# Projections of a hybrid decoder layer as a stage of their own, in seven products of halves, with attention and 22 gate chunks behind it

## The chip, the cores and the metric

The kernel runs on one core of one Trainium2 chip. The metric is device time in microseconds (us), the median of several executions. One more execution was recorded by the hardware profiler; its records are "the profile" or "the trace" here. The engines are PE (matrix products and transposes; PEld is its weight load), DVE, ACT and POOL (element-wise work), and SP, which issues most DMA transfers. ACT issues transfers too.

## The reference

One decoder layer on x of 1024 tokens by 1024 channels, float32:

```python
h = rms_norm(x, mix_norm_g)
proj = h @ w_in                      # 1024 x 8708: q, k, v of four mixers, 4 forget logits, 4 x 1024 gate logits
ys = four causal attentions of 4 heads of 64: stick-breaking (sb), dilated in 3 groups (dil),
     forgetting (fox), differential (dif)
branch = einsum('bsnc,ncd->bsnd', ys, w_branch)
x = x + sum(sigmoid(gates) * branch, axis=2) @ w_out
x = x + square(relu(rms_norm(x, mlp_norm_g) @ w_up)) @ w_down
return rms_norm(x, final_norm_g)
```

## The kernel before

**Numbers in two halves.** Every operand of a product is held as a rounded part `hi` and a rest `lo`. A product is three matmuls (`mm3`, L147 to L149): hi by hi, lo by hi, hi by lo. `wpiece` (L126, L127) makes hi and lo of a weight piece on POOL; in the MLP `split` (L966, L967) makes them on ACT and DVE.

**Stages.** (1) The normalised, transposed input `hTh`, `hTl` is made from eight tiles of x (`norm_transpose`, L178 to L186). (2) Twelve attention units run: dif 0 and 1, dil 0 to 2 with two head pairs each, fox 0 and 1, sb 0 and 1. Between them stand the projections of the next unit and the gate chunks. (3) The branch stage (`pb`) merges the four branches by gates, (4) `po` is w_out, (5) `pu` and `pd` are the MLP. The MLP already works in seven products of halves in place of eight (Strassen's scheme in Winograd's form; the table `PRODUCTS`).

**Projections.** `lin_T` makes 128 columns of q or k for all tokens: 2 halves of the tokens by 8 blocks of channels by 3 matmuls of width 512 (tile `lin`). `proj_v` makes 256 columns of v (tile `linv`, width 256). `gate_ahead` makes one of 32 gate chunks (tile `lg`, 48 matmuls of width 512) and stores it in DRAM (`gl`). q, k and v go from PSUM by `evac_hi` on ACT and `evac_lo` on DVE straight into the SBUF tiles that attention reads; only v of the dilated groups 1 and 2 goes by DRAM.

**Attention.** Per head and block of 128 queries: scores into PSUM (`sc`), a row operation on DVE (fox L576, dif L634, dil L704; sb: two sigmoids on ACT, L508 and L509, then a scan and a product on DVE, L510 and L513), `exp` on ACT, and then `pv`: transposes on PE (`pt`, L419), hi on ACT (L423), lo on DVE (L424), products with v on PE (`o`, L428 and L430). Fox also adds a row on POOL (L567) and scales by 1/sum on DVE (L583). The buffers are NS = 5 row tiles `s`, 2 PSUM tiles for scores, 2 for transposes, 1 for outputs.

**What sets the order.** The program is written unit by unit; `N_BEFORE`, `N_AFTER` and `N_MID` say how many gate chunks are written around each unit. The framework's scheduler then fixes one order per engine when the program is built, and each engine runs its list in that order. A chunk therefore need not stay where it was written.

Of the kernel before, what the change touches and what calls it, by code (L numbers as in the profile page):

```python
# [11 lines left out]
F32 = mybir.dt.float32  # L12
# [9 lines left out]
P = 128  # L22
# [20 lines left out]
N_BEFORE = (1, 4, 3, 3, 0, 0, 0, 0, 0, 1, 1, 0)  # L43
N_AFTER = (0, 1, 1, 0, 0, 0, 0, 0, 1, 0, 3, 9)
N_MID = (0, 4)
# [3 lines left out]
W_AT = 2  # L49

DW_AT = 2

UORDER = (0, 1, 2, 3, 4, 5)

ORDER_N = (3, 2, 1, 0)

NWR, NWH, NS, NPT, NQK = 4, 4, 5, 6, 12
# [4 lines left out]
def kernel(  # L62
# [111 lines left out]
    def norm_transpose(xt, rs, g_bc, t, hi, lo, xn, pspool, tag):  # L174

        if rs is None:
            rs = rms_rstd(xt, xn, D)
        nc.vector.scalar_tensor_tensor(xn, xt, rs, g_bc, op0=ALU.mult, op1=ALU.mult)  # L178
        for b in range(2):
            ps = pspool.tile([P, 4, P], F32, tag=tag, name=nm("nt"))  # L180
            for i in range(4):
                nc.tensor.transpose(ps[:, i], xn[:, (4 * b + i) * P:(4 * b + i + 1) * P], ident)
            oh = hi[:, 4 * b:4 * b + 4, t * P:(t + 1) * P]
            ol = lo[:, 4 * b:4 * b + 4, t * P:(t + 1) * P]
            nc.scalar.copy(oh, ps)
            nc.vector.tensor_sub(ol, ps, oh.bitcast(F32))  # L186

# [8 lines left out]
    hT_pool = tc.tile_pool(name="hT", bufs=1, side="right")  # L196
    hT_pool_c = ctx.enter_context(ExitStack())
    hTp = hT_pool_c.enter_context(hT_pool)
    hTh = hTp.tile([P, NK, T], F32R, name="hTh")
    hTl = hTp.tile([P, NK, T], F32R, name="hTl")  # L200


    with ExitStack() as actx:
# [6 lines left out]
        g_bc = ap_.tile([P, D], F32, tag="s", bufs=NS, name="g_bc")  # L210
        for t in range(NT):
            xt = ap_.tile([P, D], F32, tag="qk", bufs=NQK, name=nm("xt"))
            nc.sync.dma_start(xt, x[t * P:(t + 1) * P, :])
            if t == 0:
                nc.sync.dma_start(g_bc, mix_norm_g[0:1, :].to_broadcast([P, D]))
            if t == W_AT:
                ws_first = [wcols(w_in, (DIF_V, DIL_V, DIL_V + 256, DIL_V + 512, FOX_V, SB_V)[UORDER[0]], 256)]
            xn = ap_.tile([P, D], F32, tag="s", bufs=NS, name=nm("xn"))
            norm_transpose(xt, None, g_bc, t, hTh, hTl, xn, ps_t, "t")

# [45 lines left out]
        bf_row = const.tile([P, 4], F32, name="bf_row")  # L266
        nc.sync.dma_start(bf_row, b_forget[0:1, :].to_broadcast([P, 4]))
# [19 lines left out]


        plan, held = [], []

        def w_next(off, n):
            assert plan[0] == (off, n), (plan[0], off, n)
            plan.pop(0)
            return held.pop() if held else wcols(w_in, off, n)

        def w_prefetch():
            if plan and not held:
                held.append(wcols(w_in, *plan[0]))

        def lin_T(off, evac):  # L300
            ws = w_next(off, P)
            for th in range(2):
                ps = ps_lin.tile([P, 512], F32, tag="lin", name=nm("lin"))
                sl = slice(th * 512, th * 512 + 512)
                mm3(ps, [(ws[k], (hTh[:, k, sl], hTl[:, k, sl])) for k in range(NK)])
                with tc.high_priority(offset=EVAC_LEAD):
                    evac(th, ps)

        def order(ap, th, dil):

            if dil == 1:
                return ap[:, th * 512:(th + 1) * 512]
            n = 512 // dil
            return ap.rearrange("p (r n) -> p r n", r=dil)[:, :, th * n:(th + 1) * n]

        def src(ap, dil):
            if dil == 1:
                return ap
# [613 lines left out]

# [346 lines left out]
```

## Time and profile before

| | us |
|---|---|
| median of 3 runs (lowest, highest) | 1944.81 (1938.52, 1946.4) |
| profiled execution, its own time | 1943.38 |
| its span | 1941.2 |
| PE busy | 1849.6 |
| DVE, ACT, POOL busy | 1067.5, 829.6, 822.6 |

The profiled time is 2.2 us over its span and 1.4 us under the median. Matmuls overlap in the pipeline, so the mean duration of one is longer than the distance between two; the distance is what PE has to pay. A row of windows gives, for a stretch, its length, then busy time and count of PE, PEld, DVE, ACT, POOL, then the granted PE clock (1.00 is full), the share of the DMA engines and GB/s. In the groups `| a, b | c <-X d` means a us busy in total, b ns for one, c us idle of that engine before them, d of it ended by X.

### The profile page before, as it was taken

The page shows a single profiled execution, that of the slowest core. Times are in us where ns is not written, and L with a number is a line of the kernel's source. Part 1 is how long each engine was busy: PE and PEld are TensorE (multiplying, and loading weights), DVE is VectorE, ACT ScalarE, POOL GpSimd, SP SyncE. Part 2 cuts the span into 40 slices and gives each one's busy share as a digit, 9 for nine tenths or more (in the row PEclk, how much of TensorE's full clock was granted, in tenths as well). Part 3 has the DMA queues.
Part 4 walks back from the last instruction along what each step waited for, and adds up shares of the span by engine and source line. Part 5 has one row for each costly group of instructions (what it writes and reads, how often), then busy time and mean ns, then how long its engine had stood idle before and what let it go on. Part 6 is the DMA issues. An engine that isn't in the chain of part 4 may idle for free.

```text
span 1941.2 us, 27207 instructions
## 1 busy us (share of the span) xinstructions
PE 1849.6 (95%) x9635; PEld 1554.0 (80%) x9635; DVE 1067.5 (55%) x1872; ACT 829.6 (43%) x1709; POOL 822.6 (42%) x739
## 2 busy tenths in 40 slices
PE   7999999999999999999998799959999999999997
PEld 7888877888888889888886578948888887788885
DVE  5143464535444457586632684294455454859587
ACT  4133443445444344454422442255454544444354
POOL 4333244322222433332333673365565541617164
PEclk9999999999999999999998899979999999999999
DMA  4734113224242322222236953233535439665355
GB/s 146 165 93 125 49 49 88 61 86 137 60 143 62 82 60 68 55 56 66 77 93 195 302 168 138 88 114 134 165 130 165 134 120 367 213 187 179 109 175 184
DMA packets 205880, 246.99 MB, mean 127 GB/s; under 512 B 16816, under 2 KB 129840, under 8 KB 205744
## 3 DMA queue, kind: packets, MB, share of 16 engines
q1 hardware_dynamic: 166912, 168.52, 29.3%
q10 hardware_dynamic: 38832, 76.73, 11.8%
q8 instruction: 76, 1.25, 0.3%
q14 instruction: 60, 0.49, 0.1%
HBM read 166.38 MB, written 65.18 MB: 119 GB/s over the span
## 4 chain that ended last, share of the span: by engine, by line
PE 82%; DVE 6%; DMA 5%; issue 4%; POOL 2%; ACT 1%; SPq 0%; POOLq 0%; DVEq 0%; ACTq 0%
PE lg L147 6%; PE lg L148 6%; PE lg L149 6%; PE pu L1083 5%; PE pu L1084 5%; PE pu L1082 5%; PE lin L149 5%; PE lin L148 5%; PE lin L147 5%; PE pd L1187 5%; PE pd L1185 4%; PE pd L1186 4%; PE pt L419 3%; PE linv L148 2%; PE linv L147 2%
## 5 line engine op out<-in xcount | busy, mean ns | idle before, releaser
L126 POOL TENSOR_SCALAR wh<-wr 128x512 fp32r<-128x512 f32 (+1 forms) x168 | 114.6, 684 | 443.4 <-PE linv L149 144.3
L127 POOL TENSOR_TENSOR wl<-wr,wh 128x512 fp32r<-128x512 f32 (+1 forms) x168 | 233.8, 1395 | 9.1
L147 PE MATMUL lg<-hTh,wh 128*128 128x512 f32 x512 | 204.1, 399 | 2.6 <-ACT gs L483 2.6
L148 PE MATMUL lg<-hTl,wh 128*128 128x512 f32 x512 | 204.4, 399 | 0.0
L149 PE MATMUL lg<-hTh,wl 128*128 128x512 f32 x512 | 203.2, 397 | 0.0
L1185 PE MATMUL pd<-wh,sh 128*128 128x512 f32 x448 | 177.1, 399 | 3.6 <-ACT sh L966 3.5
L1186 PE MATMUL pd<-wl,sh 128*128 128x512 f32 x448 | 175.7, 396 | 0.0
L1187 PE MATMUL pd<-wh,sl 128*128 128x512 f32 x448 | 169.8, 397 | 3.5 <-DVE sl L967 3.5
L967 DVE TENSOR_TENSOR sl<-sr,sh 128x512 fp32r<-128x512 f32 x112 | 108.2, 966 | 84.8 <-ACT sh L966 84.4
L148 PE MATMUL lin<-hTl,wh 128*128 128x512 f32 x384 | 153.8, 401 | 0.0
L147 PE MATMUL lin<-hTh,wh 128*128 128x512 f32 x384 | 153.7, 400 | 0.0
L149 PE MATMUL lin<-hTh,wl 128*128 128x512 f32 x384 | 152.2, 400 | 0.0
L966 ACT CAST sh<-sr 128x512 fp32r<-128x512 f32 x112 | 69.4, 619 | 160.3 <-PE pd L1186 140.6
L424 DVE TENSOR_TENSOR ptl<-pt,pth 128x512 fp32r<-128x512 f32 (+2 forms) x168 | 99.4, 604 | 68.6 <-ACT pth L423 67.4
L423 ACT CAST pth<-pt 128x512 fp32r<-128x512 f32 (+2 forms) x168 | 85.1, 524 | 94.8 <-PE pt L419 90.4
L147 PEld LDWEIGHTS lg<-hTh,wh 128*128 128x128 f32 x512 | 96.6, 189 | 23.4 <-ACT gs L483 1.9
L147 PE MATMUL linv<-wh,hTh 128*128 128x256 f32 (+1 forms) x384 | 112.5, 295 | 1.8 <-POOL wh L126 1.7
L148 PE MATMUL linv<-wl,hTh 128*128 128x256 f32 (+1 forms) x384 | 112.4, 293 | 0.0
L149 PEld LDWEIGHTS lg<-hTh,wl 128*128 128x128 f32 x512 | 96.3, 188 | 19.9
L149 PE MATMUL linv<-wh,hTl 128*128 128x256 f32 (+1 forms) x384 | 111.7, 292 | 0.0
L148 PEld LDWEIGHTS lg<-hTl,wh 128*128 128x128 f32 x512 | 96.4, 188 | 18.8
L967 DVE TENSOR_TENSOR wl<-wq,wh 128x512 fp32r<-128x512 f32 x75 | 74.6, 994 | 56.5 <-ACT wh L966 55.2
(344 smaller groups left out, 4951.3 us busy)
## 6 DMA issues: line engine op xcount, KB each, us to landing
wr<-in_w_in_dram SPq DMA_DIRECT2D x132, 256.0 KB
br<-in_w_down_dram SPq DMA_DIRECT2D x96, 256.0 KB
gl<-gs ACTq DMA_DIRECT2D x64, 256.0 KB
sg<-gl SPq DMA_DIRECT2D x64, 256.0 KB
sr<-sa_s SPq DMA_DIRECT2D x64, 256.0 KB
wq<-in_w_up_dram SPq DMA_DIRECT2D x60, 256.0 KB
sa_s<-o ACTq DMA_DIRECT2D x48, 256.0 KB
sr<-sa_a SPq DMA_DIRECT2D x48, 256.0 KB
```

Of the source, the lines that this page charges most:

```text
L126: nc.gpsimd.tensor_scalar(hi, raw, 1.0, 1.0, op0=ALU.mult, op1=ALU.mult)
L127: nc.gpsimd.tensor_sub(lo, raw, hi.bitcast(F32))
L147: nc.tensor.matmul(ps, ah, bh, start=(i == 0), stop=False, skip_group_check=True)
L148: nc.tensor.matmul(ps, ah, bl, start=False, stop=False, skip_group_check=True)
L149: nc.tensor.matmul(ps, al, bh, start=False, stop=(i == n - 1), skip_group_check=True)
L424: nc.vector.tensor_sub(lo[:, :n], ps[:, :n], hi[:, :n].bitcast(F32))
L967: nc.vector.tensor_sub(o[1], i, o[0].bitcast(F32))
L1082: nc.tensor.matmul(ps, w_, bh[:, k], start=start and k == 0, stop=False, skip_group_check=True)
L1083: nc.tensor.matmul(ps, w_, bl[:, k], start=False, stop=False, skip_group_check=True)
L1185: nc.tensor.matmul(ps, sh[0][:, ts_], w[0], start=start and j == 0, stop=False, skip_group_check=True)
L1186: nc.tensor.matmul(ps, sh[0][:, ts_], w[1], start=False, stop=False, skip_group_check=True)
L1187: nc.tensor.matmul(ps, sh[1][:, ts_], w[0], start=False, stop=last and j == NPAIR - 1, skip_group_check=True)
```

## The change

1. **A stage of projections ahead of all attention.** v of fox and dif is made as before. Then 19 jobs follow: q with k of the 12 units, v in two pairs of keys (`wide`, matmuls of width 256), and 10 gate chunks in pairs. A job multiplies a 1024 by 1024 input by two column blocks, cut into halves by channels, tokens and column blocks: seven products of 4 blocks in place of eight (`seven`). The sums of the input's blocks (t1 to t4) are made once, beside the norm; those of the weights (s1 to s4) on POOL in each job, and split by ACT and DVE.
2. **q, k, v through DRAM.** Every result is split into hi and lo and stored by ACT's queue (`qk_d`, `v_d`). Attention loads it by SP's queue (`load_qk`, `load_dif`, `load_v`), one unit ahead. The dif units become four, one per head.
3. **Gate chunks in attention:** 22, made as before, written in numbers `N_GATE` behind the units; no weights are fetched ahead by hand.
4. **Fox** scales its rows on POOL in place of DVE. The row tiles and PSUM tiles of attention keep their numbers; `qk` has 8 tiles in place of 12 beside 4 fixed tiles `kl`, `v` 2 in place of 3.

Branch stage, w_out and MLP are unchanged.

```diff
-N_BEFORE = (1, 4, 3, 3, 0, 0, 0, 0, 0, 1, 1, 0)
-N_AFTER = (0, 1, 1, 0, 0, 0, 0, 0, 1, 0, 3, 9)
-N_MID = (0, 4)
+NG_PROJ = 5
+N_GATE = (2, 3, 2, 3, 1, 0, 1, 0, 1, 1, 1, 1, 3, 3)
...
-NWR, NWH, NS, NPT, NQK = 4, 4, 5, 6, 12
+NWR, NWH, NS, NPT, NQK = 4, 4, 5, 6, 8
...
+                xt = p0.tile([P, D], F32, tag="x", bufs=3, name=nm("xt"))
...
+                if t < NH:
+                    r = st_tile("raw", F32).rearrange("p b (k n) -> p b k n", k=NH)
+                    for b in range(2):
+                        sl = (slice(None), slice(NH * b, NH * b + NH), slice(t * P, (t + 1) * P))
+                        nc.gpsimd.tensor_add(r[:, b], hTh[sl].bitcast(F32), hTl[sl].bitcast(F32))
...
+                    nc.vector.tensor_sub(t1, pss[0], b11)
+                    nc.vector.tensor_sub(t2, pss[1], t1)
+                    to("t2", t2)
+                    to("t1", t1)
+                    nc.gpsimd.tensor_sub(b11, t2, b11)
+                    to("t3", b11, nc.gpsimd.tensor_sub)
+                    nc.gpsimd.tensor_sub(b21, b21, t2)
+                    to("t4", b21, nc.gpsimd.tensor_sub)
...
+        def seven(q, wide, out):
...
+                ws = [wsplit(i) for i in q[a_]]
+                bh, bl = hB[b_]
+                for lane in lanes:
+                    ps = pss[key][lane]
+                    for j in range(2 if wide else 1):
...
+                        for k in range(NH):
...
+                            for i, (l_, r_) in enumerate(ops):
+                                nc.tensor.matmul(o, l_, r_, start=start and j == 0 and k == 0 and i == 0,
+                                                 stop=stop and k == NH - 1 and i == 2, skip_group_check=True)
...
+            for lane, ps in enumerate(prod(0, "x", False)):
+                us.append(c_tile("u"))
+                nc.scalar.copy(us[lane], ps)
+            for lane, ps in enumerate(prod(1, "y", True)):
+                nc.vector.tensor_add(us[lane], ps, us[lane])
+            for lane, ps in enumerate(prod(2, "x", True)):
+                out(0, 0, lane, ps)
...
+        def out_qk(key, scale, dil):
...
+                evac_hi(hi, i_, sc)
+                evac_lo(lo, i_, hi, sc)
+                d = qk_d[key][c]
+                if dil == 1:
+                    nc.scalar.dma_start(d[:, :, th * H:(th + 1) * H].rearrange("s p t -> p s t"), st.bitcast(F32))
...
+        def load_qk(key, turn):
...
+                get(k[0:64], kd[0, r])
+                get(k[64:128], kd[0, r])
+                get(kl[0:64], kd[1, r])
+                get(q[0:64], qd[0, r])
+                get(q[64:128], qd[1, r])
...
+        def load_v(key, p, dil=1):
+            vt = ap_.tile([P, NT, 2, P], F32R, tag="v", bufs=2, name=nm("v"))
...
         def gate_ahead(n, dm):
...
-            w_prefetch()
...
-                            nc.vector.tensor_scalar(s[:, :w], s[:, :w], r, 1.0, op0=ALU.mult, op1=ALU.mult)
+                            nc.gpsimd.tensor_scalar(s[:, :w], s[:, :w], r, 1.0, op0=ALU.mult, op1=ALU.mult)
...
+        for i in range(len(units)):
+            cur = nxt
+            nxt = units[i + 1]() if i + 1 < len(units) else None
+            cur()
+            for _ in range(N_GATE[i]):
+                gate_ahead(*ahead.pop(0))
```

How this moves PE's list is seen at three places. The first is the last unit, sb 1, before: `pt`, `sc` and `o` are attention, `lg` is a gate chunk.

```order
L401 MATMUL sc_9812<-klB_9237,qB_9175 128x384
L506 LDWEIGHTS ident_b
L506 MATMUL sc_9812<-mask_sb,ident_b 128x128
L400 MATMUL sc_9823<-kB_9235,qB_9175 128x512
L401 MATMUL sc_9823<-klB_9237,qB_9175 128x512
L506 LDWEIGHTS ident_b
L506 MATMUL sc_9823<-mask_sb,ident_b 128x128
L149 MATMUL lg_10181<-hTh,wl_10139 128x512
L147 MATMUL lg_10181<-hTh,wh_10138 128x512
```

The same scores of sb 1 in the changed kernel, on PE:

```order
L575 MATMUL sc_10759<-kl_4687,q_9778 128x384
L673 LDWEIGHTS ident_b
L673 MATMUL sc_10759<-mask_sb,ident_b 128x128
L602 MATMUL o_10564<-pth_10627,v_9769 128x256
L574 MATMUL sc_10770<-k_9779,q_9778 128x512
L575 MATMUL sc_10770<-kl_4687,q_9778 128x512
L673 LDWEIGHTS ident_b
L673 MATMUL sc_10770<-mask_sb,ident_b 128x128
L604 MATMUL o_10564<-ptl_10628,v_9769 128x256
L602 MATMUL o_10564<-pth_10627,v_9769 128x128
```

No gate product stands there any more: attention follows attention. The second place is PE's last gate product in the changed kernel; it stands in dil 1, second head pair (`q_7425`), though six of the 22 chunks were written behind the sb units.

```order
L593 MATMUL pt_7776<-ident,s_7765 128x128 x3
L575 MATMUL sc_7816<-kl_4686,q_7425 128x128
L140 MATMUL lg_11143<-hTh,wh_11110 128x512
L141 MATMUL lg_11143<-hTl,wh_11110 128x512
L142 MATMUL lg_11143<-hTh,wl_11111 128x512
L574 MATMUL sc_7821<-k_7426,q_7425 128x256
L575 MATMUL sc_7821<-kl_4686,q_7425 128x256
L574 MATMUL sc_7845<-k_7433,q_7432 128x128
```

Behind it PE's list holds 1094 attention instructions (230 of dil, 432 of fox, 432 of sb) and no gate product. Before, a gate product or a projection stands between almost any two groups of attention. The third place is the end of attention, before:

```order
L428 MATMUL o_9859<-pth_10005,v_8200 128x256
L430 MATMUL o_9859<-ptl_10006,v_8200 128x256
L428 MATMUL o_9859<-pth_10005,v_8200 128x128
L430 MATMUL o_9859<-ptl_10006,v_8200 128x128
L149 MATMUL lg_10432<-hTh,wl_10415 128x512
L147 MATMUL lg_10432<-hTh,wh_10414 128x512
L148 MATMUL lg_10432<-hTl,wh_10414 128x512
```

The same place now, with the first products of the branch stage (`pb`):

```order
L602 MATMUL o_10806<-pth_10952,v_9769 128x256
L604 MATMUL o_10806<-ptl_10953,v_9769 128x256
L602 MATMUL o_10806<-pth_10952,v_9769 128x128
L604 MATMUL o_10806<-ptl_10953,v_9769 128x128
L140 MATMUL pb_11247<-yh_11215,wh_11236 128x512
L140 MATMUL pb_11255<-yh_11215,wh_11236 128x512
```

The 136 gate products that closed the stage before are gone from there. At the start of attention, PE's list now has 48 gate products of the first chunk (37 of them behind the last projection product), three small ones of fox's cumulated sum, and then the first score of dif; before, that score stood among projection products of the next unit.

More of the change, by code (lines that the diff above doesn't have):

```diff
@@ L286, in qk_tile @@
             return ap_.tile([P, T], F32R, tag="qk", bufs=NQK, name=nm(n))
[L289 to L307, printed above, removed]
```

477 lines of the change are left out of this document (263 added, 214 removed).

## The prediction

> **What bounds the kernel now.** The page's head and its chain of waits come first.
>
> ```profile
> span 1941.2 us, 27207 instructions
> PE 1849.6 (95%) x9635; PEld 1554.0 (80%) x9635; DVE 1067.5 (55%) x1872; ACT 829.6 (43%) x1709; POOL 822.6 (42%) x739
> PE 82%; DVE 6%; DMA 5%; issue 4%; POOL 2%; ACT 1%; SPq 0%; POOLq 0%; DVEq 0%; ACTq 0%
> ```
>
> PE carries 82% of the chain. The windows by stage say where: up to PE's first work, the start, everything to the last gate product, the gap to the first branch product, the rest.
>
> ```profile
> 0.00:8.04 8.04, 0.00 (x0) 0.00 (x0) 1.93 (x8) 2.55 (x4) 2.38 (x13) 1.00 0.76 249
> 8.04:21.00 12.96, 10.28 (x43) 8.94 (x44) 7.90 (x17) 8.92 (x17) 11.40 (x12) 1.00 0.89 315
> 21.00:1038.00 1017.00, 1002.10 (x5689) 861.24 (x5688) 510.52 (x1168) 420.93 (x961) 346.60 (x387) 0.99 0.29 82
> 1038.00:1047.80 9.80, 0.57 (x3) 0.14 (x1) 2.77 (x4) 4.64 (x8) 0.97 (x1) 0.68 0.79 272
> 1047.80:1941.20 893.40, 836.67 (x3904) 683.65 (x3904) 544.36 (x676) 392.55 (x722) 461.21 (x327) 0.97 0.54 174
> ```
>
> In the long stretch PE is busy for 1002 of 1017 us and DVE for half: attention hides behind products. The last 893.4 us are code that stays, and I leave them as they are. The change is decided in the first 1047.8 us.
>
> A product's price is its distance to the next, from stretches with one kind of product only (MLP, width 512; w_out, width 256), and for small ones from PE's timeline.
>
> ```profile
> 1200.00:1250.00 50.00, 49.57 (x417) 49.16 (x416) 5.50 (x8) 8.17 (x32) 14.83 (x16) 1.00 0.16 47
> 1350.00:1400.00 50.00, 50.00 (x216) 40.42 (x215) 24.27 (x31) 25.31 (x42) 30.77 (x23) 1.00 0.41 138
> ```
>
> ```profile
> 999.78 0.93 PE L419 MATMUL pt<-ident,sg 128*128 128x128 f32 x7
> 1000.46 0.47 PE L147 MATMUL lg<-hTh,wh 128*128 128x512 f32 x1
> ...
> 1006.60 0.23 PE L428 MATMUL o<-pth,v 128*128 128x128 f32 x1
> 1006.66 0.27 PE L430 MATMUL o<-ptl,v 128*128 128x128 f32 x1
> 1006.77 0.45 PE L149 MATMUL lg<-hTh,wl 128*128 128x512 f32 x1
> ```
>
> Width 512: 50.00 / 216 = 0.2315 us. Width 256: 49.57 / 417 = 0.119. A transpose: 0.68 / 7 = 0.10. A pair of width 128: 0.17.
>
> **Products saved.** The groups give the counts before.
>
> ```profile
> L147 PE MATMUL lg<-hTh,wh 128*128 128x512 f32 x512 | 204.1, 399 | 2.6 <-ACT gs L483 2.6
> L147 PE MATMUL lin<-hTh,wh 128*128 128x512 f32 x384 | 153.7, 400 | 0.0
> L147 PE MATMUL linv<-wh,hTh 128*128 128x256 f32 (+1 forms) x384 | 112.5, 295 | 1.8 <-POOL wh L126 1.7
> ```
>
> Three matmuls each: 2688 of width 512 and 1152 of width 256. After, by the code: 17 jobs of 7 x 4 x 3 = 84 (1428), 22 chunks of 48 (1056); 2 wide jobs of 336 and 384 direct ones of width 256. Saved: 204 x 0.2315 + 96 x 0.119 = 47.2 + 11.4 = 58.6 us. Attention's own PE work stays: 572 transposes 57, output products (448 of width 256, 248 of 128) 53 + 21, scores (120 of 512, 72 of 384 at three quarters of 0.2315, 160 of 256, 128 of 128) 28 + 12.5 + 19 + 11, masks and norm some 5: 207 us. Before, 622 + 137 + 207 + 6 for the input's transposes = 972 of 1047.8 us; in the long stretch about 967 of 1017, that is 95%. So if PE stayed as full as that, 59 us would be won. It doesn't; five stages follow.
>
> **Stage 1, projections: 486 us.** Work: 6 + 126 (1056 of width 256) + 331 (1428 of 512) = 463. One job (19.4 us of PE) needs on DVE 7 splits, 5 sums and 4 rests.
>
> ```profile
> L967 DVE TENSOR_TENSOR wl<-wq,wh 128x512 fp32r<-128x512 f32 x75 | 74.6, 994 | 56.5 <-ACT wh L966 55.2
> L1229 DVE TENSOR_TENSOR x<-x,pd 128x512 f32<-128x512 f32 x24 | 15.2, 679 | 4.9 <-PE pd L1187 4.9
> ```
>
> That is 7 x 0.99 + 5 x 0.68 + 4 x 0.68 to 0.99 = 13 to 14.3 us, beside PE; the MLP, with the same splits, keeps PE at 50.00 of 50 (the row of 1350). Transfers are 1 MB in and 2 MB out per job, 155 GB/s, under the 315 that the start reached. The start loses what it lost before, 8.0 us to PE's first work and some 11 more to its first full stretch: the input's transposes ran to 41.7 us there.
>
> ```profile
> L182 PE MATMUL nt<-ident,xn 128*128 128x128 f32 x64 | 12.2, 329 | 9.0 <-DVE xn L178 8.0 <-DVE ss L162 0.9
> ```
>
> The sums t1 to t4 add about 3.5 us of DVE and 5.6 of POOL per tile of x in the second half; 384 products (46 us) are there to cover them, but in the list only 144 stand ahead of the last transposes. I take 19 us for the start and 4 for stalls: 486; ends 478 and 498.
>
> **Stage 2, handover: 10 us.** The first unit's 1 MB of v and sixteen transfers of 128 KB land in memory that projections free last. 3 MB at 249 to 315 GB/s (rows above) are 10 to 12 us; 37 gate products, 8.6 us, cover them, and then the chain score, row, exp, transpose starts empty. The distance tables, built at the very start before, now stand here too, beside the transfers. The trace has no such place, so 10 lies between 4 (all covered) and 20 (nothing covered).
>
> **Stage 3, attention with gates: 344 us.** 1045 gate products, 242, and 40% of attention, 85: 327 at 95% is 344. DVE was busy for half of the long stretch before, so I take PE as the bound here too. Weights come by SP's queue behind the loads of q and k, and those wait for PE to free tiles; the fetch ahead is gone. Ends, my choice around 95%: 334 at 98%, 359 at 91%.
>
> **Stage 4, attention alone: 258 us.** This is the step that decides. Behind the last gate product stand 1094 attention instructions (230 of dil, all of fox and sb). Their PE work is 122 us, so PE is no longer the bound; the other engines are. Groups of fox (a window's answer) and of sb:
>
> ```profile
> L424 DVE TENSOR_TENSOR ptl<-pt,pth 128x512 fp32r<-128x512 f32 (+1 forms) x41 | 25.3, 629 | 10.1 <-ACT pth L423 9.8
> L583 DVE TENSOR_SCALAR s<-s,r 128x128 f32<-128x128 f32 (+7 forms) x32 | 21.6, 675 | 0.6
> L576 DVE CUSTOM_DVE_ANT_0 s<-sc,s 128x512 f32<-128x512 f32 (+3 forms) x32 | 18.2, 570 | 14.6 <-POOL s L567 8.7 <-PE sc L401 4.5 <-PE sc L574 0.9
> L576 DVE CUSTOM_DVE_ANT_0 s<-sc,s,mn 128x256 f32<-128x256 f32 (+2 forms) x16 | 9.2, 577 | 5.7 <-PE sc L574 5.4
> L439 DVE TENSOR_TENSOR y<-o,otmp 64x512 f32<-64x512 f32 x8 | 5.4, 678 | 0.8 <-ACT otmp L436 0.7
> L582 DVE RECIPROCAL r<-l 128x1 f32<-128x1 f32 x32 | 5.2, 162 | 16.1 <-ACT s L580 15.6
> ```
>
> ```profile
> L510 DVE TENSOR_TENSOR_SCAN kp<-kp,zero_col 128x128 f32<-128x128 f32 (+7 forms) x32 | 46.5, 1456 | 5.7 <-ACT kp L508 5.5
> L513 DVE TENSOR_TENSOR sg<-sg,kp 128x128 f32<-128x128 f32 (+7 forms) x32 | 29.9, 934 | 5.9 <-ACT sg L509 3.2 <-POOL kp L499 0.7
> ```
>
> Fox keeps 25.3 + 18.2 + 9.2 + 5.4 + 5.2 = 63 us on DVE, and some 4 for reading its minima; its 21.6 of scaling go to POOL, which has time but takes them in order: the row sums of the next blocks (L567) queue behind a scale that waits for DVE's reciprocal. Sb has 46.5 + 29.9 + 25.3 + 5.4 = 107. Together 174 us. How full can DVE be without cover? One stretch of before is pure attention, 108 instructions of dil in a row:
>
> ```profile
> 443.60:461.30 17.70, 15.11 (x112) 13.07 (x111) 13.90 (x51) 14.92 (x48) 0.00 (x0) 1.00 0.12 45
> ```
>
> DVE 13.90 of 17.70 us, 79%; ACT 84%. With five row tiles and two PSUM tiles each way the chain leaves a fifth idle, and sb, which takes two row tiles per block, is no better placed. 174 / 0.785 = 222; dil by the same row, 230 x 17.70 / 112 = 36. Sum 258. Low end: DVE never idle, 174 + 230 x 13.90 / 112 = 203. High end: 310, below. Loads hide: 3.5 MB per dil unit of about 15 us is 233 GB/s, under 315; if not, 3 us per unit.
>
> A drop of PE's clock is the danger here. The trace shows one inside attention:
>
> ```profile
> 549.90:553.30 3.40, 1.77 (x11) 1.32 (x11) 3.40 (x11) 3.33 (x14) 0.00 (x0) 1.00 0.19 64
> 553.30:556.80 3.50, 3.50 (x19) 3.50 (x19) 1.70 (x4) 1.76 (x4) 0.00 (x0) 0.51 1.01 341
> ```
>
> With 11 instructions in 3.4 us the clock fell to half for the next 3.4; with 112 in 17.7 it stayed at 1.00. Stage 4 has 1094 in 258, about 14 per 3.4 us, between the two. I put a few drops into the 258 and the rest into a rival.
>
> The Trainium skill, "TensorE: Matmul & The Clock Gate", Part 4: PE-mode transpose, says that transposes do not count as PE activity for the full clock; by that rule nearly a third of stage 4's products would not hold the clock, and the sum would go to the rival's. The pure stretch, transposes included, kept 1.00, so this trace does not bear the rule out there.
>
> **Stage 5, to the branch stage: 6 us.** Before 9.8 us (1038.0 to 1047.8), as branch weights waited for the buffers of the last gates. They are now fetched during sb; y of dif is long stored, but its tiles need attention's memory.
>
> **Sum.** 486 + 10 + 344 + 258 + 6 = 1104 against 1047.8: 56 us more. The profiled execution took 1943.4, so 2000 in its terms; it lies 1.4 under the median of 1944.8, so 2001 for the median.
>
> **The rivals.** *The clock falls in stage 4 and stays low.* PE's 122 us become up to 244 at half clock, nearly what DVE needs with its waits, and each row then waits for two slow engines in turn: 310 for stage 4, 2053. For it: 14 instructions per 3.4 us, and stretches of sb with long scans. Against: at half clock PE is soon fully busy, and the row at 553.3 shows it back after 3.4 us. *No change.* DVE runs without gaps in stage 4, 203 in place of 258: 1049, 1946. For it: POOL is nearly idle and PE's queue short; against: the 79%. *Faster.* The engines don't wait for each other at all behind the projections: no handover, gates and attention at 100%, DVE full: 486 + 327 + 203 + 6 = 1022, 26 us less, 1919. It decides when attention, from the last projection product to the first branch product, takes under 551 us against 618 in my sum and 536 in this case. Against: 95% is what PE reached with cover everywhere. *Gates do stand beside sb on the chip.* The list is fixed when the program is built, so I give that nothing.
>
> **How the numbers follow.** Forecast 0.70, low clock 0.16, no change 0.08, faster 0.06. A measurement of this kernel can tell about 0.5%, 10 us, from no change. Forecast and low clock are slower: 0.86; same 0.08; faster 0.06. All low ends of the stages together, with 203 in stage 4: 478 + 4 + 334 + 203 + 6 = 1025; all high ends: 498 + 20 + 359 + 310 + 10 = 1197. They won't meet; the range leaves out "faster" and the lower half of "no change" below, and the worst sums above: 1950 to 2050.
>
> **What would show it.** Right: the first score near 490 us; the last gate product (`lg`) near 840; behind it some 250 us in which PE's work is half of the time, DVE is busy for about 80%, and the waits name ACT and DVE of attention; `pb` near 1104; from there 893 us as before. Wrong: `pb` before 1050, DVE over 95% in the stretch without gates, or projections that take over 500 us because PE waits for DVE's splits or for transfers.

## The result and the profile after

The changed kernel takes 2085.31 us (median of 4 runs, 2082.93 to 2089.7), the kernel before 1941.66 in the same session: a ratio of 1.074, 95% interval 1.0707 to 1.0774. The sign was forecast, the size was not: 2001 with a range to 2050. The profiled execution took 2085.09 us for a span of 2083.4.

The page's head and its chain of waits, after:

```profile
span 2083.4 us, 27428 instructions
PE 1884.4 (90%) x9335; PEld 1554.3 (75%) x9335; DVE 1230.5 (59%) x2076; ACT 909.4 (44%) x1846; POOL 822.2 (39%) x695
PE 68%; DVE 10%; DMA 8%; issue 5%; ACT 4%; POOL 3%; SPq 1%; ACTq 0%; POOLq 0%; DVEq 0%
```

PE's share of the chain fell from 82% to 68%; DVE, DMA, ACT and POOL took it over. The windows after, cut at the first and the last projection product, the first score, the last gate product, the last attention product and the first branch product (columns as before):

```profile
0.00:92.00 92.00, 66.42 (x449) 63.95 (x450) 48.49 (x95) 36.52 (x82) 67.46 (x66) 0.91 0.45 139
92.00:504.90 412.90, 412.90 (x2112) 349.25 (x2111) 248.58 (x341) 145.84 (x254) 124.35 (x85) 1.00 0.50 149
504.90:517.00 12.10, 9.66 (x44) 7.42 (x43) 5.29 (x18) 3.32 (x8) 3.35 (x4) 0.96 0.57 171
517.00:914.00 397.00, 359.95 (x1737) 292.45 (x1738) 187.00 (x516) 172.13 (x392) 112.26 (x116) 0.92 0.46 124
914.00:1182.40 268.40, 200.87 (x1096) 159.36 (x1094) 190.31 (x428) 154.63 (x384) 57.78 (x104) 0.83 0.40 104
1182.40:1193.50 11.10, 0.25 (x4) 0.10 (x2) 0.71 (x2) 2.46 (x5) 0.00 (x0) 0.62 0.57 189
1193.50:2083.40 889.90, 834.34 (x3904) 681.80 (x3904) 550.07 (x680) 394.51 (x725) 457.01 (x320) 0.97 0.54 174
```

| stage | forecast | measured | off by |
|---|---|---|---|
| 1, projections | 486 | 504.9 | +18.9 |
| 2, handover | 10 | 12.1 | +2.1 |
| 3, attention with gates | 344 | 397.0 | +53.0 |
| 4, attention alone | 258 | 268.4 | +10.4 |
| 5, to the branch stage | 6 | 11.1 | +5.1 |
| rest | 893.4 | 889.9 | -3.5 |

The errors sum to 86.0 us, and more than half of them lie in stage 3. The jobs themselves ran as worked out: 412.9 us for a work of 411, PE full at a clock of 1.00, so the count of products behind the 59 us of saving holds. What was lost stands on both sides of them.

**The start.** POOL's groups up to 93 us, and PE's waits up to 95 us:

```profile
L277 POOL TENSOR_TENSOR raw<-hTh,hTl 128x512 f32<-128x512 f32 x8 | 13.1, 1647 | 0.6 <-DVE hTl L189 0.6
L120 POOL TENSOR_TENSOR wl<-wr,wh 128x520 fp32r<-128x520 f32 (+1 forms) x8 | 10.9, 1382 | 0.1
L293 POOL TENSOR_TENSOR raw<-raw,tt 128x512 f32<-128x512 f32 x4 | 6.9, 1717 | 0.0
L189 POOL TENSOR_TENSOR t3l<-raw,t3h 128x512 fp32r<-128x512 f32 x4 | 6.5, 1626 | 0.0
L291 POOL TENSOR_TENSOR raw<-tt,raw 128x512 f32<-128x512 f32 x4 | 6.0, 1493 | 3.4 <-DVE tt L288 3.4
L189 POOL TENSOR_TENSOR t4l<-raw,t4h 128x512 fp32r<-128x512 f32 x4 | 5.1, 1263 | 0.0
```

```profile
PE nt L270 <- DVE xt L265: 9.6, 3, 8.1
PE linv L140 <- DVE fl L247: 4.9, 1, 4.9
PE linv L141 <- POOL wl L120: 4.2, 1, 4.2
PE linv L140 <- POOL wh L119: 3.9, 2, 3.1
```

The sums of the input's blocks cost POOL 13.1 + 6.9 + 6.5 + 6.0 + 5.1 = 37.6 us. The forecast counted four tiles at 5.6 and overlooked the first row, 13.1 us for putting hi and lo together again. The splits of the weights of v stand behind them in POOL's order, and PE waits for these (4.2 and 3.9). The first row of the waits is no loss of the change: its longest part, 8.1 us, is PE's wait for its first work, 8.0 before.

**Stage 3.** A part of the loss has a visible cause. PE's largest wait in it, and the pieces of the chain of waits that belong to it (start, length, what):

```profile
PE lg L140 <- POOL wh L119: 11.6, 5, 3.1
```

```profile
722.55 5.97 DMA wr<-in_w_in_dram
...
782.42 6.46 DMA wr<-in_w_in_dram
...
888.24 6.62 DMA wr<-in_w_in_dram
```

Gate weights stand in SP's order behind the loads of the next unit (L527), and those wait for PE to free their tiles: in these 397 us SP's queue stands at L527 for 175 us until a score, a transpose or an output product on PE is done (80.4, 37.3, 32.6 and 24.9). But 11.6 us don't make 53. What else is lost shows in no single wait; that is what the experiments had to find.

**Stage 4** split at the first row operation of fox (978.6 us):

```profile
914.00:978.60 64.60, 44.05 (x231) 38.95 (x230) 34.58 (x126) 33.47 (x121) 8.16 (x10) 0.67 0.94 242
978.60:1182.40 203.80, 156.81 (x866) 120.41 (x866) 155.74 (x304) 121.17 (x263) 49.62 (x95) 0.88 0.22 61
```

Two errors of opposite sign met in the forecast's 258, so its nearness to 268.4 is luck. Dil took 64.6 where 36 were worked out, at a DMA share of 0.94 and a clock of 0.67. Fox and sb took 203.8 where 222 were. DVE is 76% busy there, close to the 78.5% that was used, but its busy time is 155.74 us and not 174: the 174 added up groups, whose instructions overlap a little, while the 78.5% counts DVE's busy time without overlap.

### The profile page after: what moved, and what is told of

Same layout as the page of the kernel before. It is cut to its first block, busy times and chain, and to the rows that moved or that the text cites. A ratio compares the mean times of both kernels' runs of the same rounds, so it can differ in the third digit from the quotient of the medians.

```text
span 2083.4 us, 27428 instructions
## 1 busy us (share of the span) xinstructions
PE 1884.4 (90%) x9335; PEld 1554.3 (75%) x9335; DVE 1230.5 (59%) x2076; ACT 909.4 (44%) x1846; POOL 822.2 (39%) x695
## 4 chain that ended last, share of the span: by engine, by line
PE 68%; DVE 10%; DMA 8%; issue 5%; ACT 4%; POOL 3%; SPq 1%; ACTq 0%; POOLq 0%; DVEq 0%
PE lin L350 20%; PE pu L1167 5%; PE pu L1168 5%; PE pu L1166 5%; PE pd L1271 4%; PE pd L1270 4%; PE pd L1269 4%; PE lg L140 4%; PE lg L142 4%; PE lg L141 4%; PE pt L593 2%; PE o L604 2%; DVE kp L677 1%; DMA sg<-gl 1%; PE o L602 1%
## 5 line engine op out<-in xcount | busy, mean ns | idle before, releaser
L140 PE MATMUL lg<-hTh,wh 128*128 128x512 f32 x352 | 146.9, 418 | 11.6 <-POOL wh L119 11.6
L142 PE MATMUL lg<-hTh,wl 128*128 128x512 f32 x352 | 140.0, 413 | 0.0
L602 PE MATMUL o<-pth,v 128*128 128x256 f32 (+1 forms) x348 | 106.5, 314 | 35.2 <-ACT pth L597 9.1
L188 ACT CAST wh<-wq 128x512 fp32r<-128x512 f32 x125 | 77.5, 620 | 131.3 <-PE lin L350 57.2
L120 POOL TENSOR_TENSOR wl<-wr,wh 128x512 fp32r<-128x512 f32 (+1 forms) x84 | 117.5, 1402 | 4.0
L604 PE MATMUL o<-ptl,v 128*128 128x256 f32 (+1 forms) x348 | 105.2, 336 | 15.2 <-DVE ptl L598 13.9
L602 PEld LDWEIGHTS o<-pth,v 128*128 128x128 f32 x348 | 75.0, 216 | 46.6 <-ACT pth L597 30.5
L1271 PEld LDWEIGHTS pd<-wh,sl 128*128 128x128 f32 x448 | 84.2, 188 | 26.6 <-DVE sl L189 7.3
L1269 PEld LDWEIGHTS pd<-wh,sh 128*128 128x128 f32 x448 | 84.1, 188 | 25.0 <-ACT sh L188 5.2
L1270 PEld LDWEIGHTS pd<-wl,sh 128*128 128x128 f32 x448 | 84.2, 188 | 19.6 <-DVE wl L189 0.2
L604 PEld LDWEIGHTS o<-ptl,v 128*128 128x128 f32 x348 | 75.1, 216 | 28.3 <-DVE ptl L598 26.0
```

What stands on the lines that cost most here:

```text
L120: nc.gpsimd.tensor_sub(lo, raw, hi.bitcast(F32))
L140: nc.tensor.matmul(ps, ah, bh, start=(i == 0), stop=False, skip_group_check=True)
L142: nc.tensor.matmul(ps, al, bh, start=False, stop=(i == n - 1), skip_group_check=True)
L188: nc.scalar.copy(o[0], i)
L602: nc.tensor.matmul(o_ps[:, c0:c0 + w], v, hi[:, c:c + w], start=st, stop=False, skip_group_check=True)
L604: nc.tensor.matmul(o_ps[:, c0:c0 + w], v, lo[:, c:c + w], start=False, stop=sp, skip_group_check=True)
```

## The experiments

"Attention time" below is the time from the last projection product to the first branch product: 688.6 us in the changed kernel (1193.5 - 504.9). Where nothing else is said, a time is that of one execution; the kernel before took 1941.4 to 1942.5 (medians) beside them. The four executions of the changed kernel lie within 7 us, so a smaller difference between two single ones is not read as an effect.

### Do gates beside all of attention win the time back?

The first theory said that stage 4 wastes PE, and that gate products would hide there.

```diff
-            for _ in range(N_GATE[i]):
-                gate_ahead(*ahead.pop(0))
+        def fill(n):                      # called behind each block of queries
+            marks.append(last[-1].ins)
+            for _ in range(n):
+                with tc.issue_after(marks[-2 if len(marks) > 1 else -1]):
+                    gate_ahead(ahead[0], HALF[0] % 2)
...
```

> The 22 gate chunks are held back by issue order on PE: two halves stand ahead of the first score, then 16 halves go to the four dif units, 6 to dil, 8 to fox and 12 to sb. Nothing else changes. Theory (attention without gate products leaves PE idle, and PE's work of 460 us in gates and attention could hide most of it): the time from the last projection product to the first branch product falls from 688 us to 520 to 560, and the median to 1915 to 1960. Rival (attention is set by its own loads and by its chain on DVE, ACT and POOL, with or without gates beside it): that time stays above 640 us and the median above 2035.

It took 2098.06 us (4 runs; ratio to before 1.0796, 1.0773 to 1.0819), attention 697.6 us. Its window:

```profile
508.80:1206.40 697.60, 571.82 (x2874) 456.91 (x2873) 380.80 (x962) 331.41 (x786) 174.13 (x224) 0.88 0.43 116
```

The theory fell: the cover was spread, and nothing was won. The length of each unit shows why (worked out from the trace, from one unit's last output sum on DVE to the next one's, the first from the first score; "dil" is all six units of it; in brackets the gate and projection products inside, at 0.2315 us for width 512 and 0.119 for width 256):

```
              dif 00   dif 01   dif 10    dif 11   dil        fox 0     fox 1    sb 0     sb 1
before        95 (81)  62 (46)  105 (78)  66 (52)  243 (169)  113 (81)  81 (54)  80 (53)  83 (59)
changed       71 (40)  63 (45)  95 (59)   59 (33)  177 (56)   55 (0)    50 (0)   48 (0)   48 (0)
spread        68 (26)  55 (20)  81 (22)   47 (21)  156 (33)   70 (22)   65 (22)  70 (33)  64 (33)
all in proj.  51 (0)   46 (0)   65 (0)    40 (0)   153 (0)    55 (0)    50 (0)   49 (0)   48 (0)
```

A unit of dif, fox or sb takes some 40 to 65 us by itself, and in the changed and the spread kernel products beside it lengthen it by 0.3 to 0.7 of their own time; dil paid 24 us for 56 and 3 for 33. Over all units it is about half in both kernels: 109 us for 233, and 119 for 232. What spread took from dif and dil it gave to fox and sb.

### What does a product beside attention cost?

All gates in the projection stage (the row "all in proj." above), none there, and 528 products more beside stage 4:

```diff
-NG_PROJ = 5
+NG_PROJ = 16        # all in projections; in the other run 0
```

```diff
+                with tc.issue_after(marks[-2]):
+                    ps = ps_f.tile([P, 512], F32, tag="f", name=nm("fill"))
+                    for i in range(24):
+                        nc.tensor.matmul(ps, hTh[:, i % 8, 0:128], hTh[:, i // 4, 0:512], ...)
```

> All 32 gate chunks in the projection stage (11 more jobs of 19.4 us, 214 us), none beside attention: this measures attention alone. Theory of the chain: a unit of dif takes 45 to 55 us alone, dil 20, fox 52, sb 48, so attention takes 510 to 570 us with its handover and the total is 2125 to 2190. The prediction's view (DVE 79% full when alone: 377 us / 0.785 = 480): 2075 to 2105. If products beside attention were free, attention alone would take as long as with them, 688 us, and the total 2290.

> No gate chunk in the projection stage, all 32 beside attention (5 jobs of 19.4 us less, 10 chunks of 11.1 us more). Theory from the runs so far (attention alone takes 582 us, and with 22 chunks, 233 us of products beside it, 688: a product beside attention costs about half of its own time, wherever it stands): -97 + 111 x 0.47 = -45 us, total 2030 to 2050. The prediction's view (gates and attention are bound by PE at 95%): -97 + 111 / 0.95 = +20 us, total 2095 to 2115.

> Beside dil 1 and 2, fox and sb stand 528 more matmuls of width 512 (122 us of PE at 0.2315), whose result nobody reads; the gates keep two PSUM tiles of three. The stretch from the last gate product to the last attention product was 268 us at a clock of 0.83. Theory (DVE, ACT and waits set this stretch, PE has about 139 us to spare and its clock costs little): it stays at 255 to 285 us, and the time within 20 us of 2085. Rival 1 (the low clock is what costs): the clock goes to about 1.00 and the stretch to 235 us or less. Rival 2 (PE's list sets it, every product more delays attention): the stretch grows to 330 us or more.

All in projections: 2189.43 us; no gate there: 2058.76; with the 528 products: 2152.83. The windows of attention of the first two:

```profile
718.50:1300.30 581.80, 400.88 (x1829) 309.33 (x1827) 372.62 (x961) 308.55 (x742) 85.74 (x137) 0.71 0.39 101
```

```profile
407.50:1169.80 762.30, 660.96 (x3354) 539.14 (x3352) 387.03 (x963) 345.14 (x807) 210.55 (x264) 0.92 0.44 121
```

| products beside attention, us of PE | attention time | cost per us of product |
|---|---|---|
| 0 (all in projections) | 581.8 | |
| 244 (changed kernel, 22 chunks) | 688.6 | 0.44 |
| 356 (none in projections, 32 chunks) | 762.3 | 0.51 |
| 366 (22 chunks and 528 products) | 753.7 | 0.47 |

So attention alone takes 581.8 us, 12 over the 510 to 570 expected of the chain and far over the 480 of a DVE at 79%: DVE is 64% busy in this row. Products beside it neither are free nor cost their full time, they cost about half. Without gates in projections 26.5 us came off in place of 45: the total of 2058.76 lies between what the two theories expected. The last ten chunks cost 73.7 us for 111, or 0.66, so the price rises as the cover fills up; half is a mean and no constant. The 528 products stretched stage 4 from 268.4 to 336.3 us, which is the outcome set down for PE's list as the bound, yet at 0.56 of their 122 us and not in full.

How a hidden product costs time is seen in fox and sb, in what ACT and DVE wait for; first the changed kernel (no products there), then the kernel with 100 of the 122 us there:

```profile
ACT pth L597 <- PE pt L593: 26.8, 27, 3.6
ACT otmp L610 <- PE o L604: 8.5, 9, 1.3
DVE ptl L598 <- ACT pth L597: 14.5, 22, 2.1
```

```profile
ACT pth L598 <- PE pt L594: 65.4, 22, 4.3
ACT otmp L622 <- PE o L605: 30.9, 10, 5.7
DVE ptl L599 <- ACT pth L598: 53.1, 24, 4.1
```

PE runs its list in order, so a transpose stands behind the products listed ahead of it. ACT's copy waits for the transpose, 65.4 us in place of 26.8, and DVE for ACT, 53.1 in place of 14.5. PE does not wait more for its own inputs: its longest wait in the first of these stretches, 12.7 us for `ptl`, is 1.9 in the second, where it is busy for 239.13 of 268.6 us. DVE's work is the same, 155.74 and 157.41 us; the relay is longer.

### Is it so in the kernel before?

Half of each gate chunk's products were left out there:

```diff
-mm3(ps, [(ws[k], (hTh[:, k, sl], hTl[:, k, sl])) for k in range(NK)])
+mm3(ps, [(ws[k], (hTh[:, k, sl], hTl[:, k, sl])) for k in range(NK // 2)])
```

> The kernel before, with half of each gate chunk's products left out (768 of width 512, 178 us of PE). Some 183 of them belong to the gate products that stand behind the last attention in the list (42 us). If PE bounds attention there, as the prediction read it at 95%: all 178 us come off, total 1755 to 1775. If a product beside attention costs about half of its time also here: 42 + 136 x 0.53 = 114 us come off, total 1815 to 1845.

1840.09 us, as expected of the half: 101.7 off for 178 us of products, 0.57 per us. From the first score to the last gate product, the kernel before (first) and this one:

```profile
80.60:1037.70 957.10, 942.20 (x5323) 808.07 (x5322) 489.13 (x1125) 407.02 (x932) 326.11 (x364) 0.99 0.28 81
```

```profile
82.70:896.10 813.40, 769.59 (x4409) 657.82 (x4408) 463.46 (x1089) 385.42 (x888) 321.33 (x352) 0.97 0.33 94
```

The two stretches don't hold the same work. Before, 136 gate products, 31.6 us, stand behind the last attention product at 1007 us, where they cost their full time; in the second kernel the list came out otherwise, none stand there, and 40 us of attention alone follow the last gate product. (The expectation had put 42 us of the missing products at that end.) From the first score to the last attention product the time falls from 926.4 to 853.4 us, 73 us for about 145 us of products fewer, or 0.50: half again. PE's share falls from 98% to 94% there.

That PE was full before was thus a property of the amount of cover (some 704 us of products beside 207 of attention: the 759 of the forecast less about 55 ahead of the first score), and no constant that holds for less of it.

### Why does attention alone take 582 us?

In the dif units of the kernel with all gates in projections (first score to its end) DVE is 62% busy; the window, and what DVE waits for there:

```profile
733.90:935.00 201.10, 123.84 (x408) 84.41 (x408) 124.31 (x350) 91.63 (x192) 26.72 (x32) 0.60 0.29 72
```

```profile
DVE r L780 <- ACT s L778: 32.5, 46, 1.4
DVE ptl L598 <- ACT pth L597: 14.3, 17, 2.2
DVE s L785 <- POOL s L783: 12.8, 19, 1.4
```

That is a relay: 32.5 us for `exp` on ACT, 14.3 for copies of transposed rows, 12.8 for POOL's scale. The chain of work that ended last shows the same, by line, first for the dif units here, then for 100 to 300 us of the kernel before (the view shows the beginning of each list):

```profile
by line: ACT s L778 22.1%; DVE s L773 19.5%; PE pt L593 7.9%; DVE s L785 7.9%; issue 7.0%; POOL s L783 6.8%; DVE ptl L598 4.4%; ACT pth L597 3.6%; PE o L604 3.5%; DVE r L780 3.1%; PE o L602 2.0%; DMA dm<-qk_d 1.8%; PE sc L772 1.4%; DVE y L6
by line: PE lg L147 17.8%; PE lg L148 17.6%; PE lg L149 17.4%; PE sc L633 5.5%; PE lin L149 4.7%; PE lin L148 4.3%; PE pt L419 4.3%; PE lin L147 4.2%; PE linv L147 2.9%; PE linv L149 2.9%; PE o L430 2.9%; PE linv L148 2.8%; PE o L428 2.2%; 
```

Alone, no engine carries the chain: of the lines shown DVE has 35%, ACT 26%, PE 15% and POOL 7%. Before, gate products alone made 53% of it.

In dif the bias holds one of the five row tiles. A second one holds the distance table `dist`, which is read for the last time at 883.1 us, when the bias of the last dif unit is made. So three are left in the first three dif units and four in the last; a block of 256 queries writes four. The trace agrees: at most three rows are in flight at once in the first three units and four in the last, which is also the shortest (40 us in the table).

The Trainium skill, "Perfetto Trace Analysis", section Roofline, says that with low use of both the products and HBM a kernel is bound by latency, that is, by stalls and dependencies. Attention alone as a whole fits that, with PE's work of 207 us (the prediction's count) in 582 and a DMA share of 0.39.

More row tiles, first in the changed kernel, then with other gate plans, then in attention alone:

```diff
-NWR, NWH, NS, NPT, NQK = 4, 4, 5, 6, 8
+NWR, NWH, NS, NPT, NQK = 4, 4, 7, 6, 8        # in attention alone: 12 and 8 for NS and NPT
```

> Seven row tiles in place of five in attention, nothing else written differently. New theory (attention is a chain of steps, each engine waiting for the next, with too few rows in flight: in dif one of five tiles holds the bias, so four are left, which is just one block of queries): dif and sb units overlap their blocks better, the time from the last projection product to the first branch product falls from 688 to 600 to 650 us, the total to 2000 to 2050. Rival (the engines' own work and PE's clock set attention, buffers do not): less than 10 us of change.

> The 22 chunks spread over all units by issue order, with seven row tiles. Theory (a product costs about half of its time at any place): within 20 us of seven row tiles alone, 2040 to 2072. Rival (the spread chunks did not pay only because too few rows were in flight to use them): 1980 to 2020.

> All 32 gate chunks beside attention, and seven row tiles in place of five. Seven row tiles alone took 34 us off. If the two gains add: 2005, within 1995 to 2020. If the row tiles gain only where gate products are few: 2025 to 2045.

> All gates in projections, attention alone as in the run with 582 us, but with 12 row tiles in place of 5 and 8 tiles for transposed rows in place of 6 (the input's tiles are given free for them). If too few rows in flight make attention a chain: 582 falls to 440 to 500 us and the total to 2045 to 2105; DVE is then 75 to 85% busy. If waits that tiles do not remove set it (loads, clock, PSUM): above 540 us, total above 2145.

> The same with three PSUM tiles for scores in place of two and two for outputs in place of one. If PSUM is the next limit once rows are many: another 20 to 50 us off. If not: within 15 us of twelve row tiles alone.

Seven tiles: 2051.69 us, attention 650.0, at the upper edge of what was expected (the total is 2 us past it); spread with seven: 2058.09, attention 657.9, so spreading the gates wins nothing here either; no gates in projections with seven: 2023.11. That is 62.2 under the changed kernel, so the two gains (33.6 and 26.5) add, though the total is 3 us over the range that was given for it. Twelve tiles alone: 2147.08, attention 533.8; with more PSUM tiles: 2144.27, 527.7. The windows with seven tiles and with twelve alone:

```profile
505.70:1155.70 650.00, 556.14 (x2874) 449.70 (x2872) 379.48 (x962) 331.16 (x787) 172.89 (x226) 0.91 0.46 125
```

```profile
717.20:1251.00 533.80, 382.43 (x1829) 300.25 (x1827) 365.25 (x961) 307.25 (x742) 84.86 (x137) 0.72 0.42 109
```

Rows in flight are one cause: with the tiles for transposed rows 48 of 582 us, and 39 of 689 with gates. They are not the whole one: 440 to 500 were expected, 533.8 came, with DVE at 68%. Another part stands at seams that no tile removes. With five row tiles 15.4 us go from the last projection product to the first score, which waits for its loads; 24.0 from the last row operation begun for one head pair of dif (816.4 us) to the first of the next (840.4), where the last rows drain and the output is normalised; and 10.6 from the last output product to the branch stage. With twelve tiles the same three take 15.6, 24.4 and 6.9: some 50 us of 582 and 47 of 534.

The next suspect was PE's clock, 0.72 in that row. Products right behind each score, where PE was thought to have nothing to do, were to keep it up:

```diff
+                                    fill(q, k, slice(i * P, i * P + P), 6)
```

> Attention alone with 12 row tiles, and behind each score product 6 (dil: 3) more matmuls of width 256 whose result nobody reads: 1440 of 0.119 us, 171 us of PE, 0.36 to 0.71 us at a place. If the low clock makes most of the remaining wait: the clock rises above 0.9 in the stretch, and attention falls from 534 to 450 to 505 us in spite of the products added. If the chain of the other engines makes it: the added products cost, 534 grows to 545 to 620 us. Between 505 and 545 the two cancel.

> The same products added to attention alone with 5 row tiles (582 us). Low clock: 510 to 555 us. Chain: 595 to 680 us; a cost near half of the 171 us would give 668. Between 555 and 595 the two cancel.

2220.36 us with attention 609.5, and 2280.72 with 670.5:

```profile
718.20:1327.70 609.50, 485.80 (x3269) 437.65 (x3267) 369.83 (x961) 308.14 (x740) 86.55 (x137) 0.87 0.37 96
```

```profile
719.70:1390.20 670.50, 512.19 (x3269) 452.35 (x3267) 373.22 (x961) 310.09 (x742) 85.77 (x137) 0.83 0.34 87
```

Both lie in the range of the chain. The clock rose from 0.72 to 0.87 and from 0.71 to 0.83, and the time rose as well, by 75.7 and 88.7 us for 171 of products: 0.44 and 0.52, the same half again. Raising the clock this way does not pay. How much the low clock itself takes is not separated: if every added product cost its full 0.119 us, the higher clock gave back 95 and 82 us, and it did not reach 1.00. That is an estimate: 18% of the 534 us, but more than half of the 169 us in which DVE is idle there.

### Small parts

```diff
-        nc.gpsimd.tensor_scalar(hi, raw, 1.0, 1.0, op0=ALU.mult, op1=ALU.mult)
-        nc.gpsimd.tensor_sub(lo, raw, hi.bitcast(F32))
+            nc.scalar.copy(hi, raw)                          # start: weights of v of fox and dif
+            nc.vector.tensor_sub(lo, raw, hi.bitcast(F32))
```

> The weights of v of fox and dif are split by ACT and DVE in place of POOL; POOL keeps the sums of the input's blocks. Theory (the sums on POOL hold up these splits, and PE waits for them at 60 and 64 us): the first stretch of back-to-back projection products begins at 82 to 86 us in place of 93, and the time falls by 7 to 11 us. Rival (DVE, 9 to 10 of 10 us busy from 38 to 58 us, sets the start): it begins at 91 us or later, and the time stays within 4 us.

The first job began at 81.6 us in place of 92.0, as the theory of POOL's queue has it; the time was 2089.61, so the fall of 7 to 11 us in the total did not come. The 10.4 us were lost again in attention (699.6 us in place of 688.6). Why attention is longer by 11 us is not settled.

```diff
+            if (g, pr) == (0, 0):
+                state["dil"] = (load_v("dil0", 0), *load_qk(("dil0", 0), 0))
+            v, q, k, kl = state["dil"]
...
-            q, k, kl = load_qk((key, pr), pr)
+            q, k, kl = load_qk((key, pr), pr + 1)
```

> Left out: the loads of q, k and v of five of the six dil units; all six work on the tiles of the first one (17.5 MB less). From the last gate product to the first score of fox the changed kernel took about 70 us, where 36 were predicted. Theory (these units wait for their loads, and the DMA engines are full there): that stretch falls to 35 to 45 us and the time by 25 to 40 us. Rival (the chain between the engines and the low clock): the stretch stays above 60 us and the time within 10 us of the changed kernel.

2067.19 us. From the last gate product to fox's first row operation (expected 35 to 45):

```profile
909.50:963.70 54.20, 43.99 (x238) 38.98 (x238) 35.20 (x131) 34.74 (x125) 3.73 (x5) 0.70 0.43 122
```

54.2 us in place of 64.6, so the loads make a third of the 28.6 us by which dil missed its forecast there, 18 us in all. The result lies between the two theories; the rest stays at a clock of 0.70 and is not separated into the chain and the clock.

```diff
-                            nc.gpsimd.tensor_scalar(s[:, :w], s[:, :w], r, 1.0, op0=ALU.mult, op1=ALU.mult)
+                            nc.vector.tensor_scalar(s[:, :w], s[:, :w], r, 1.0, op0=ALU.mult, op1=ALU.mult)
```

> Fox scales its rows on DVE again (one part of the change undone). Prediction's view (DVE sets fox alone): 32 scales of 0.675 us at 79% add 20 to 27 us. Theory of the chain: a step of 0.9 to 1.4 us on POOL becomes one of 0.68 us on DVE, and the row sums on POOL no longer queue behind it: fox units are 0 to 15 us faster together.

> Two PSUM tiles for attention's outputs in place of one, two for gate products in place of three. Theory of the chain of rows: outputs change hands once in two blocks of queries, so little: 0 to 15 us faster. Rival (the single output tile holds up the next half until DVE has copied it): 48 changes of hands at 0.7 to 1.5 us each, 30 to 70 us faster.

Fox's scale on DVE: 2086.28 us, the two fox units 115 us in place of 105. That is under half of what a DVE-bound fox would have lost, and against the theory of the chain, which expected a gain; other units took the 10 us back. The gain rested on a step of 0.9 to 1.4 us on POOL, but POOL's scale takes 0.37 to 1.12 us in the changed kernel, 0.74 in the median, no more than DVE's 0.68. Two output tiles: 2085.62, no change.

### A version faster than both

```diff
-NWR, NWH, NS, NPT, NQK = 4, 4, 5, 6, 12
+NWR, NWH, NS, NPT, NQK = 4, 4, 6, 6, 11        # in the kernel before
```

> The kernel before with six row tiles in place of five, and 11 tiles for q and k in place of 12. Its PE slots are 96% full while attention runs (921 of 960 us), so at most a part of the other 39 us can come off: 1925 to 1942, ratio to the kernel before 0.992 to 1.000. If rows in flight limit it as much as the changed kernel (7 tiles: 38 us in attention): 1905 to 1925.

1928.9 us (4 runs; ratio to before 0.9937, 0.992 to 0.9953), inside the first expectation: a small gain of 0.6%, clear of the noise. From the first score to the last gate product it takes 10.3 us less:

```profile
80.40:1027.20 946.80, 939.35 (x5326) 805.45 (x5324) 483.07 (x1125) 403.81 (x931) 329.39 (x364) 1.00 0.29 82
```

## Why the prediction was wrong, point by point

- **Stage 3 is the step that failed.** "327 at 95% is 344", with the reason that DVE was busy for half of the long stretch, "so I take PE as the bound". Measured 397.0, with PE's slots filled for 327 / 397 = 82%; 37 of the 1045 gate products stand ahead of the first score and were counted in stage 2 already, so it is rather 318 / 397 = 80%. DVE was busy for 47% of this stage too (187.00 of 397), so a half-busy DVE does not show that PE is the bound. The 95% belonged to a stretch with 704 us of products beside attention. With 244, what bounds is the relay between the engines: attention alone takes 582 us, and the other runs add 0.44 to 0.53 us per us of product (0.53 is the 528 products' 65.1 us for 122), which makes 689 to 711 for stages 2 to 5. Measured are 688.6, forecast were 10 + 344 + 258 + 6 = 618: 71 of the 86 us missed.
- **Stage 4 was near in its sum by luck and off in its parts**: 268.4 for 258, from 28.6 us too little for dil and 18.2 too much for fox and sb. The share of 79% nearly held for fox and sb (76%); the 174 us that it divided were too many. The dil row of 17.70 us for 112 instructions came from a place with a DMA share of 0.12 and a clock of 1.00; here 0.94 and 0.67 stood beside them.
- **Stage 1**: the jobs were right to a few us (412.9). The start took 92.0 us, where 52 of work and 19 of loss were counted: 13.1 us of POOL's sums were put at nothing, and the order on POOL put the sums ahead of weights that PE needs. The run with the splits moved off POOL shows 10.4 us of it; the rest is open, with a clock of 0.91 in the start. The prediction's sign of being wrong, over 500 us for this stage, came true, but through POOL's order and not through DVE's splits or transfers, as it had said.
- **Stages 2 and 5**: 12.1 for 10 and 11.1 for 6.
- **The low clock** was a rival at 0.16 with 310 us for stage 4. The clock did fall, to 0.83 in stage 4 and 0.92 in stage 3, and the total passed even that rival's 2053; but stage 4 took 268. The rival's place and price were wrong; what the clock costs in stage 3 is not separated.
- **"Faster"** turned on attention taking under 551 us against 618. Even with no gate product beside it, it takes 582.
- **The range** left out the sum of all high ends, 1197, because they "won't meet". The stages came to 1193.5, but not by meeting: stages 2 and 4 stayed inside their ends, stages 1 and 5 passed them a little, and stage 3 passed its end of 359 by 38 us. That end, 91%, was a choice around a share that did not hold.
- **Where the 59 us of saved products went**: before, all weight products not needed at the start lay beside attention at about 0.55 us per us ((1047.8 - 80.6 - 582) / 704; 0.50 by the halved gates). This is an estimate: the 582 us were measured in the changed kernel, whose attention has loads that the kernel before does not have. In their own stage the products cost their full time, 413 us, while DVE is busy for 60% of it and ACT for 35%, and attention can't use what is left.

Open: what part of the 534 us with twelve row tiles is the low clock, what the order that is fixed at build time, and what the loads at unit starts beyond the seams above. That the relay bounds attention is shown by its own time, by the waits and by the price of products beside it; how its 582 us divide is shown only in part.

## What to carry to other kernels

Measure the stage that is to be left alone (here 582 us) before pricing the work beside it: a fill rate read from a stretch with plenty of cover doesn't carry over to one with a third of it. A product put beside a chain of engines wasn't free and wasn't full price here; it cost about half of its time in the sum of each run and 0.66 for the last ten chunks, so spreading the gates won nothing and their number counted. Splitting this kernel into a full stage and a waiting stage gave up the overlap that the full stage could have lent. And count what else lives in a pool of tiles: a table read once per unit held a row tile through most of dif.

## What was not expected of the hardware

- Products put right behind the scores of attention alone, where PE's work fills 207 of 582 us, still cost 0.44 to 0.52 of their time (171 us added, 75.7 and 88.7 paid), though they raised the clock from 0.72 to 0.87 and from 0.71 to 0.83.
- The granted clock in attention alone was 0.71 over 582 us, and 0.60 in dif. PE was recorded as busy for 400.88 of the 582 us, for work of about 207 at the prices of the full clock: here busy time doesn't tell how much work was done.
- DVE's rests of 128 x 512 in the start, in the groups up to 93 us, where POOL is busy for 73%:

```profile
L189 DVE TENSOR_TENSOR hTl<-nt,hTh 128x512 fp32r<-128x512 f32 x16 | 10.6, 681 | 1.1 <-ACT hTh L188 1.0
L189 DVE TENSOR_TENSOR t2l<-tt,t2h 128x512 fp32r<-128x512 f32 x4 | 5.1, 1278 | 0.1
L189 DVE TENSOR_TENSOR t1l<-tt,t1h 128x512 fp32r<-128x512 f32 x4 | 4.0, 1006 | 0.0
```

Read from PSUM (`nt`) a rest took 0.68 us, read from SBUF (`tt`) beside POOL's work 1.28 and 1.01. Two more of the same size read from SBUF, begun at 90.8 and 91.6 us while POOL does nothing, took 0.69 and 0.68. That speaks for POOL as the cause; no run tests it.
